# Neighbours on TensorE: linear attention's state products next to its value sums, retention's value sums next to the next pair's scores

## The chip, the cores and the metric

The kernel runs on one core of one Trainium2 chip. A core has a matrix engine (TensorE, PE in the profile), a vector engine (VectorE, DVE), an activation engine (ScalarE, ACT), a general one (GpSimd, POOL) and a queue engine (SyncE, SP), each with its own instruction stream. The metric is the device time of one execution in microseconds (us), the median of the runs.

## The reference

Two layers of a hybrid decoder trunk over 1024 positions of width 1024, all in float32. Each layer makes one projection of the normalised input and cuts it into three head groups: sliding-window attention, retention and gated linear attention. The two that the change touches are recurrences over chunks:

```python
# retention: 4 heads, chunk 128, head width 64
sc = jnp.einsum('bhid,bhjd->bhij', qi, ki) * dmask          # scores
intra = jnp.einsum('bhij,bhjv->bhiv', sc, vi)               # value sums
inter = jnp.einsum('bhid,bhdv->bhiv', qi * q_decay, state)  # inter-chunk product
new_state = chunk_decay * state + jnp.einsum('bhjd,bhjv->bhdv', ki * k_decay, vi)  # state product

# gated linear attention: 4 heads, chunk 64, key width 32, value width 64
sc = jnp.einsum('bhid,bhijd,bhjd->bhij', qi, decay, ki)
intra = jnp.einsum('bhij,bhjv->bhiv', sc, vi)
inter = jnp.einsum('bhid,bhdv->bhiv', qi * jnp.exp(b), state)
new_state = jnp.exp(b_last) * state + jnp.einsum('bhjd,bhjv->bhdv', ki * jnp.exp(b_last - b), vi)
```

Each head's output is RMS-normalised and multiplied by a gate; the three groups are joined, projected by `w_out`, normalised and added to the input.

## The kernel before

The 1024 positions are eight tiles of 128, worked in four pairs (`p` = 0 to 3, tiles 2p and 2p+1). Both recurrences use chunks of 128 positions, one a tile. A projection is a chain of 24 products: the float32 operands are split into two rounded parts and three of their four cross products are summed into one accumulator bank. Most such products have 512 output columns; in the profile they are the groups with output `mm`.

TensorE's order is the program's own. The program is a planner: `mult` issues a product and advances a clock `clk` by its planned cost. The projections are the main line. Everything else is a generator (a "job") that yields a delay, or a delay and the name of a flag; `pump()`, called every few products of a projection, resumes each job whose time has come and whose flag has been set long enough. A job's products so land between the products of a projection. The delays stand in the table `L`, by name and, with `@1`, for layer 1; `lat("rc3", l)` reads one, and `flag(name, lat)` says that something will be ready after `lat`. They order the work and enforce nothing: real waits are semaphores. The other engines' orders come from the framework's scheduler.

Products that don't fill the 128 rows and 128 columns of the array use a part of it: a product over 64 rows (retention's scores, one head each), one with 64 output rows, which uses 64 of the array's columns (`within`, the value sums of retention and of linear attention, and the attention's), one that uses 32 columns (linear attention's state products). The profile shows this as rows*columns: `64*128`, `128*64`, `128*32`.

Accumulators are eight banks: three for projections (`mm()`), five for everything else (`aux()`, 8 - MMB). A bank comes free when its last reader is through. Working tiles in SBUF come from pools too: 14 of width 512 (`t2`) and 7 of width 256 (`t1`).

The functions that the change touches:

- `within(po, i, v, sc)`: four products for one tile, two heads side by side, summed into the output bank `po`. The first starts the bank's accumulation.
- `gla_core` (linear attention, one pair): operands; then the scores of both tiles, masked into `scz`; then the state products `pst`, in 32 columns each; then the delays `gc3` and `gc4`; then the value sums; then for each tile the inter-chunk product (from the state copy `stG`) and VectorE's state update.
- `ret_core` (retention, one pair): waits for the turned operands of both tiles (`rT`), issues the scores of both, VectorE multiplies them with the causal mask into `sc`; after the delay `rc3` come the value sums, and then for each tile the inter-chunk product (from `stR`), the state product and VectorE's update of `stR`; then it starts the output job.
- `ret_out` and `head_norm_gate`: norm and gate of a pair's output from the bank `po`, stored to DRAM for the output projection, which reads it much later.

Lines that the prediction names: L171 every product, L186 every transpose, L147 ScalarE's copies, L967 attention's masked copy out of a score bank, L1253 retention's mask, L1273 and L1275 the update of `stR`, L635 the scaling of the normed input, L1223 the last step of retention's rotation, L1149 to L1166 linear attention's operands.

Of the kernel before, what the change touches and what calls it, by code (L numbers as in the profile page):

```python
# [17 lines left out]
P = 128  # L18
# [4 lines left out]
NP_ = NT // 2  # L23
# [66 lines left out]
def trunk(ctx: ExitStack, tc: tile.TileContext, ins, cst, out):  # L90
# [35 lines left out]
    def aux(dt=F32):  # L126
        return ps.tile([P, 512], dt, tag="aux", name=nm("aux"), bufs=8 - MMB)
# [34 lines left out]
    def h4(ap):  # L162
        return ap.rearrange("p (h q) -> p h q", h=4)
# [640 lines left out]
    stR = cp.tile([P, 2, P], F32, name="stR")  # L804
# [336 lines left out]
    def gla_core(l, p, qk, vs):  # L1141

        yield (lat("gc1", l), ("dec", l, p))
        dA, dB, dC, g = dec[(l, p)]
        flag(("dec0", l, p))
        kxz, kdz, qx, qd, scz = gz["kx"], gz["kd"], gz["qx"], gz["qd"], gz["sc"][p % 2]
        k = qk[:, 256:512]
        a1, ad = t2(), t2()
        V.tensor_tensor(a1, qk, dA, ALU.mult)  # L1149
        V.tensor_tensor(ad, qk, dB, ALU.mult)  # L1150
        q1, k1 = a1[:, 0:256], a1[:, 256:512]
        for s, src in enumerate((dC[:, 0:64], dC[:, 64:192], dC[:, 192:384])):
            n = 8 * s + 8
            eng(f"kd{s}").tensor_tensor(b32(kdz[:, s])[:, :, 0:n], b32(k)[:, :, 0:n],
                                        src.rearrange("p (b i) -> p b i", i=n), ALU.mult)
        kds = [kdz[:, 0], kdz[:, 1], kdz[:, 2], ad[:, 256:512]]
        for s in range(4, 0, -1):
            kv_ = kxz[:, s - 1].rearrange("p c (b i) -> p c b i", i=32)
            eng(f"kx{s}").tensor_tensor(kv_[:, :, 0:s, :], cb32(k1)[:, :, 0:s, :],
                                        g[:, :, 4 * s:5 * s].unsqueeze(3).to_broadcast((P, 2, s, 32)), ALU.mult)  # L1160
        qb = t1()
        eng("qb").tensor_tensor(cb32(qb), cb32(q1), g[:, :, 20:24].unsqueeze(3).to_broadcast((P, 2, 4, 32)), ALU.mult)
        for h in range(4):
            r = slice(32 * h, 32 * h + 32)
# [7 lines left out]
        A.activation(kbn, pt[:, 0:256], AF.Copy)  # L1172
# [12 lines left out]
        pst = aux()  # L1185
        for c in range(2):
            if 2 * p + c < NT - 1:
                for h in range(4):
                    mult(pst[32 * h:32 * h + 32, 64 * c:64 * c + 64], kbn[:, c * P + 32 * h:c * P + 32 * h + 32],
                         vs[c][:, 64 * h:64 * h + 64], True, True, 0.03)  # L1190
        yield lat("gc3", l)
        yield lat("gc4", l)
        po = aux()
        for c in range(2):
            within(po, c, vs[c], scz[c])
        for c in range(2):
            t = 2 * p + c
            if c:
                yield lat("gc6", l)
            if t > 0:  # L1200
                yield (0.0, ("stG", l, t))
            if t > 0:
                for j in range(2):
                    mult(po[:, 256 * j + P * c:256 * j + P * c + P], stG[:, 2 * j:2 * j + 2, :].rearrange("p h d -> p (h d)"),
                         qb[:, c * P:(c + 1) * P], False, c == 1 and j == 1)
            if t < NT - 1:
                V.scalar_tensor_tensor(stC, stC, g[:, c, 24:25], pst[:, 64 * c:64 * c + 64], ALU.mult, ALU.add)
                eng("stx").tensor_tensor(stG, stC.unsqueeze(1).to_broadcast((P, 4, 64)),
                                         hmask.unsqueeze(2).to_broadcast((P, 4, 64)), ALU.mult)
                flag(("stG", l, t + 1), lat("gc5", l))  # L1210
        job(gla_out(l, p, po))
# [26 lines left out]
    def ret_core(l, p, ks, vs):  # L1238
        ts = (2 * p, 2 * p + 1)
        for t in ts:  # L1240
            yield (0.0, ("rT", l, t))
        qT = [turned[(l, t)][:, 0:256] for t in ts]
        kT = [turned[(l, t)][:, 256:512] for t in ts]
        sp = [aux(), aux()]
        for i in range(2):
            for h in range(4):
# [3 lines left out]
        sc = [t2(), t2()]  # L1250
        for i in range(2):
            for c in range(2):
                V.tensor_tensor(h4(sc[i])[:, c:4:2], sp[c][:, 256 * i:256 * i + 256].rearrange("p (h q) -> p h q", h=2),  # L1253
                                causal.unsqueeze(1).to_broadcast((P, 2, P)), ALU.mult)
        yield lat("rc3", l)
        po = aux()
        for i, t in enumerate(ts):
            within(po, i, vs[i], h4(sc[i]))
        for i, t in enumerate(ts):
            if t > 0:  # L1260
                yield (0.0, ("stR", l, t))
            if t > 0:
                for j in range(2):
                    mult(po[:, 256 * j + P * i:256 * j + P * i + P], stR[:, j, :], qT[i][:, j * P:(j + 1) * P], False, i == 1 and j == 1)
            if t < NT - 1:
                pst = aux()
                for j in range(2):
                    mult(pst[:, j * P:(j + 1) * P], ks[i][:, j * P:(j + 1) * P], vs[i][:, j * P:(j + 1) * P],
                         True, True)
                for c in range(2):  # L1270
                    r = slice(64 * c, 64 * c + 64)
                    blk = stR[r, :, 64 * c:64 * c + 64]
                    V.tensor_tensor(blk, blk, pst[r, 0:256].rearrange("p (j n) -> p j n", j=2)[:, :, 64 * c:64 * c + 64],  # L1273
                                    ALU.add)
                V.tensor_tensor(stR, stR, cdt.unsqueeze(2).to_broadcast((P, 2, P)), ALU.mult)  # L1275
                flag(("stR", l, t + 1), lat("rc4", l))
        job(ret_out(l, p, po))

    def ret_out(l, p, po):
# [523 lines left out]
L = {"tt1": 5.86, "tt2": 6.96, "tb1": 28.02, "tb2": 0.05, "pf3": 12.26, "pf1": 6.83, "pf2": 2.88, "mod1": 3.75, "mod2": 2.4, "mod3": 17.58, "mod4": 0.67, "mod5": 0.05, "mod6": 0.05, "pre1": 7.76, "kv1": 15.26, "kv2": 2.17, "aq1": 11.36, "aq7": 4.15, "ag1": 5.72, "aq2": 1.11, "aq6": 7.35, "aq3": 11.35, "aq4": 7.65, "aq5": 2.86, "hn1": 3.34, "hn2": 10.67, "gz1": 9.1, "gz2": 13.49, "gl1": 5.15, "gd3": 17.16, "gc1": 1.82, "gc2": 1.95, "gc3": 0.62, "gc4": 4.49, "gc6": 2.54, "gc5": 4.23, "rc1": 6.33, "rc2": 0.05, "rc3": 1.29, "rc4": 3.27, "fin1": 10.23, "lay1": 0.05, "mod2@1": 2.23, "mod3@1": 15.08, "mod5@1": 2.83, "mod6@1": 3.24, "pre1@1": 10.18, "kv1@1": 4.49, "kv2@1": 0.16, "aq1@1": 6.75, "aq7@1": 7.39, "ag1@1": 10.22, "aq2@1": 2.07, "aq6@1": 9.39, "aq3@1": 11.41, "aq4@1": 6.32, "aq5@1": 1.56, "hn1@1": 4.35, "hn2@1": 9.0, "gz1@1": 5.99, "gz2@1": 8.59, "gl1@1": 20.55, "gd3@1": 15.63, "gc1@1": 2.47, "gc2@1": 4.67, "gc3@1": 0.54, "gc4@1": 0.84, "gc6@1": 1.27, "gc5@1": 0.05, "rc1@1": 5.87, "rc2@1": 2.37, "rc3@1": 2.6, "rc4@1": 5.96, "fin1@1": 6.8, "lay1@1": 0.15, "gc7": 1.43, "gc7@1": 0.05, "tb0": 1.39, "mod7": 1.05, "mod7@1": 1.25}  # L1803
CHUNK = 7
VDB = 8
VDF = 6
# [50 lines left out]
```

## Time and profile before

| | |
|---|---|
| median of 3 runs | 951.92 us (950.53 to 952.58) |
| the profiled execution | 952.01 us |
| its span, first to last instruction | 950.3 us |
| granted TensorE clock, mean | 0.995 |
| TensorE busy | 926.2 us, 97% |
| VectorE, ScalarE, GpSimd busy | 71%, 52%, 24% |

Layer 0's retention stands at about 113 to 205 us of the span, its linear attention at 215 to 300; in layer 1 at 575 to 677 and 677 to 761. In a timeline row a group's length includes the time that its last product takes to pass through the array, so it overlaps the next group; the time from one group's start to the next one's is what the group took of the engine. An idle time in brackets stands with the instruction that ended it.

### The profile page before, as it was taken

The numbers are of one execution on the slowest core, as the hardware profiler recorded it, in microseconds if no ns is written. First come the engines' busy times: TensorE is split into PE (matmuls) and PEld (weight loads), VectorE is DVE, ScalarE is ACT, GpSimd is POOL, SyncE is SP. The second block draws the span as 40 slices with busy tenths as digits, with TensorE's granted clock in tenths as the row PEclk, the third lists the DMA queues.
The fourth block names the chain that finished last, engine by engine and source line by source line (L and its number), as shares of the span: only waits on it lengthen the run. The fifth ranks groups of instructions, "written<-read, shape, count | busy, mean of one in ns | idle before, by whom it ended". The sixth has DMA issues, their size and how long they took to land.

```text
span 950.3 us, 15898 instructions
## 1 busy us (share of the span) xinstructions
PE 926.2 (97%) x5561; PEld 759.8 (80%) x5561; DVE 671.9 (71%) x1426; ACT 496.9 (52%) x1196; POOL 226.7 (24%) x290
## 2 busy tenths in 40 slices
PE   5999999999999999999999999999999999999897
PEld 1699877878898777778889888888889887777685
DVE  6886857848686988655487474784667588678775
ACT  2686333553766766633356441343667577746442
POOL 3222000332240324420123110023233033532000
PEclk8999999999999999999999999999999999999999
DMA  9943623523353245688545251252124133467653
GB/s 329 316 136 104 180 72 124 175 80 112 111 169 112 89 125 178 209 250 280 187 168 184 75 161 60 89 179 88 41 82 124 48 93 99 142 206 224 208 180 111
DMA packets 120206, 140.18 MB, mean 148 GB/s; under 512 B 11727, under 2 KB 86841, under 8 KB 120125
## 3 DMA queue, kind: packets, MB, share of 16 engines
q1 hardware_dynamic: 111964, 129.00, 42.9%
q10 hardware_dynamic: 8160, 10.15, 3.1%
q8 instruction: 44, 0.72, 0.3%
q14 instruction: 38, 0.30, 0.1%
HBM read 105.56 MB, written 33.55 MB: 146 GB/s over the span
## 4 chain that ended last, share of the span: by engine, by line
PE 82%; DMA 6%; DVE 5%; issue 3%; ACT 2%; POOL 1%; SPq 1%; DVEq 0%; POOLq 0%; ACTq 0%
PE mm L171 65%; PE aux L171 13%; PE aux L186 4%; DMA st<-in_w_in_dram 1%; DMA aoS<-t 1%; DMA t<-mixF 1%; DMA xk<-in_x_dram 1%; DMA wm<-in_w_mod_dram 1%; DVE t L339 0%; DMA t<-in_x_dram 0%; DVE arena L1327 0%; POOL arena L509 0%; DMA wide<-in_w_out_dram 0%; ACT smx L972 0%; ACT t L147 0%
## 5 line engine op out<-in xcount | busy, mean ns | idle before, releaser
L171 PE MATMUL mm<-arena,arena 128*128 128x512 f32 (+2 forms) x1392 | 287.5, 359 | 0.0
L171 PE MATMUL mm<-arena 128*128 128x512 f32 (+2 forms) x1392 | 284.6, 358 | 0.3 <-ACT arena L709 0.3
L171 PEld LDWEIGHTS mm<-arena 128*128 128x128 f32 x1392 | 227.4, 189 | 37.7 <-issue 1.2
L171 PEld LDWEIGHTS mm<-arena,arena 128*128 128x128 f32 x1392 | 227.2, 189 | 37.5 <-issue 2.1
L171 PE MATMUL mm<-arena,mx 128*128 128x512 f32 x624 | 146.9, 392 | 2.4 <-ACT wide L1432 2.4
L171 PEld LDWEIGHTS mm<-arena,mx 128*128 128x128 f32 x624 | 115.9, 188 | 27.8 <-ACT wide L1432 2.8
L509 POOL TENSOR_TENSOR arena<-st,arena 128x512 fp32r<-128x512 f32 x53 | 79.9, 1514 | 158.8 <-ACT arena L147 92.2
L147 ACT ACTIVATE t<-aux 128x512 f32<-128x512 f32 x64 | 36.8, 590 | 75.0 <-PE aux L171 36.5
L147 ACT ACTIVATE arena<-st 128x512 fp32r<-128x512 f32 x82 | 48.4, 624 | 31.6 <-PE mm L171 19.8
L972 ACT ACTIVATE smx<-smx,sm 128x129 f32<-128x129 f32 x128 | 50.1, 394 | 21.5 <-DVE sm L969 21.2
L509 DVE TENSOR_TENSOR arena<-st,arena 128x512 fp32r<-128x512 f32 x55 | 54.0, 997 | 7.8 <-ACT arena L147 4.7
L385 DVE SCALAR_TENSOR_TENSOR acc<-st,c_act,acc 128x512 f32<-128x512 f32 x60 | 46.6, 776 | 14.9 <-DMA st<-in_w_mod_dram 13.8
L976 POOL TENSOR_TENSOR smx<-smx,sm 128x512 f32<-128x512 f32 x32 | 35.8, 1118 | 83.2 <-DVE sm L975 79.4
L563 POOL TENSOR_TENSOR sm<-sm,few 128x1 f32<-128x1 f32 x27 | 16.8, 622 | 140.7 <-DVE sm L562 127.6
L186 PE MATMUL aux<-c_ident,t 128*128 128x128 f32 x224 | 34.5, 279 | 4.5 <-DVE t L635 2.7
L967 DVE COPY_PREDICATED smx<-c_curmask,aux 128x256 f32<-128x256 int32 x64 | 25.5, 447 | 14.9 <-ACT smx L147 13.6
L186 PEld LDWEIGHTS aux<-c_ident,t 128*128 128x128 f32 x224 | 27.4, 143 | 10.8 <-DVE t L635 3.2
L371 POOL MEMSET acc<- 128x512 f32 x4 | 2.1, 529 | 133.2 <-PE aux L171 119.1
L1028 DVE TENSOR_TENSOR t<-t,t 128x512 f32<-128x512 f32 x16 | 11.3, 708 | 29.3 <-ACT t L1027 26.2
L852 DVE TENSOR_TENSOR t<-mm,sincos 128x128 f32<-128x128 f32 (+2 forms) x36 | 16.2, 449 | 22.4 <-ACT t L147 12.4
L655 ACT ACTIVATE t<-aux,mod,mod 128x128 f32<-128x128 f32 x56 | 21.2, 455 | 19.5 <-PE aux L186 17.5
L1535 DVE SCALAR_TENSOR_TENSOR t<-t,sm,t 128x512 f32<-128x512 f32 x27 | 20.6, 786 | 13.3 <-DMA t<-in_x_dram 9.5
(278 smaller groups left out, 1479.4 us busy)
## 6 DMA issues: line engine op xcount, KB each, us to landing
st<-in_w_in_dram SPq DMA_DIRECT2D x96, 256.0 KB, 3.2
st<-in_w_mod_dram SPq DMA_DIRECT2D x64, 256.0 KB, 3.6
st<-in_w_out_dram SPq DMA_DIRECT2D x40, 256.0 KB, 3.1
mx<-mixS SPq DMA_DIRECT2D x20, 512.0 KB, 4.9
mixS<-t SPq DMA_DIRECT2D x36, 256.0 KB, 2.2
wm<-in_w_mod_dram SPq DMA_DIRECT2D x12, 512.0 KB, 5.3
t<-in_x_dram SPq DMA_DIRECT2D x24, 256.0 KB, 5.0
t<-tabS SPq DMA_DIRECT2D x16, 256.0 KB, 3.6
```

Source lines behind the costliest of these rows:

```text
L147: A.activation(dst, src, AF.Copy)
L171: T.matmul(dst, lhsT, rhs, start=start, stop=stop, skip_group_check=more)
L186: T.transpose(dst, src, idn)
L385: V.scalar_tensor_tensor(acc, wt, c_act[:, k:k + 1], acc, ALU.mult, ALU.add)
L509: i = (G if first == 0 and kc in LOG else V if first == 0 else eng(f"wlo{kc}")).tensor_tensor(wt[:, 1, 2 * kc:2 * kc + 2, 0:256], st, f(hi ...
L563: after[2] = G.tensor_tensor(r, r, mhalf[:, :w], ALU.pow)
L655: A.activation(hf[:, ks], pt[:, ks], AF.Identity, scale=gain, bias=shift)
L852: V.tensor_tensor(a4, s4, cs.unsqueeze(1).unsqueeze(1).to_broadcast((P, nh, 2, 32)), ALU.mult)
L967: V.copy_predicated(sv, curmask.unsqueeze(1).to_broadcast((P, 2, P)), pv[:, :, n // P - 1, :])
L972: A.activation(sm[:, h, :], sm[:, h, :], AF.Exp, bias=mx[:, h:h + 1], accum_out=sums[:, h:h + 1])
L976: eng("pn").tensor_tensor(sm[:, :, 0:128], sm[:, :, 0:128], rs.unsqueeze(2).to_broadcast((P, 4, P)), ALU.mult)
L1535: V.scalar_tensor_tensor(xt[j], yg[j], r, xt[j], ALU.mult, ALU.add)
```

## The change

In linear attention the state products move from ahead of the delays `gc3` and `gc4` to behind them, directly ahead of the value sums. In retention the value sums of a pair are taken out of its `ret_core`: the output bank is started by the inter-chunk product instead, and the bank, the masked scores and the values are kept in `waiting`. The next pair's `ret_core` issues the kept value sums directly ahead of its own scores; the last pair issues its own after a wait on the flag `rsc`, set `rc3` after the scores. The output job starts after the value sums. No product is added or taken away.

```diff
-    def within(po, i, v, sc):
+    def within(po, i, v, sc, start=True, stop=False):
...
-                     not i and not j, False, 0.108)
+                     start and not i and not j, stop and j == 1, 0.108)
...
@@ gla_core @@
+        yield lat("gc3", l)
+        yield lat("gc4", l)
+        po = aux()
         pst = aux()
         for c in range(2):
             if 2 * p + c < NT - 1:
                 for h in range(4):
                     mult(pst[32 * h:32 * h + 32, 64 * c:64 * c + 64], ...)
-        yield lat("gc3", l)
-        yield lat("gc4", l)
-        po = aux()
         for c in range(2):
             within(po, c, vs[c], scz[c])
...
@@ ret_core @@
         kT = [turned[(l, t)][:, 256:512] for t in ts]
+        if waiting:
+            yield (0.0, ("rsc", l, p - 1))
+            ret_within(l, *waiting.pop())
         sp = [aux(), aux()]
...
-        yield lat("rc3", l)
+        flag(("rsc", l, p), lat("rc3", l))
         po = aux()
-        for i, t in enumerate(ts):
-            within(po, i, vs[i], h4(sc[i]))
+        first = True
         for i, t in enumerate(ts):
             if t > 0:
                 yield (0.0, ("stR", l, t))
             if t > 0:
                 for j in range(2):
-                    mult(po[...], stR[:, j, :], qT[i][...], False, i == 1 and j == 1)
+                    mult(po[...], stR[:, j, :], qT[i][...], first, False)
+                    first = False
...
+        waiting.append((p, po, vs, sc))
+        if p == NP_ - 1:
+            yield (0.0, ("rsc", l, p))
+            ret_within(l, *waiting.pop())
+
+    waiting = []
+
+    def ret_within(l, p, po, vs, sc):
+        for i in range(2):
+            within(po, i, vs[i], h4(sc[i]), False, i == 1)
         job(ret_out(l, p, po))
```

Of the table `L`, these delays change (planner's us). Layer 0, or both layers where there is no entry of its own for layer 1: `tt2` 6.96 to 5.77, `tb1` 28.02 to 32.23, `pf3` 12.26 to 12.47, `pf2` 2.88 to 3.57, `mod3` 17.58 to 14.64, `mod6` 0.05 to 3.45, `kv2` 2.17 to 5.43, `aq1` 11.36 to 11.16, `aq7` 4.15 to 9.71, `ag1` 5.72 to 4.63, `aq3` 11.35 to 10.06, `aq5` 2.86 to 5.44, `gl1` 5.15 to 9.88, `gd3` 17.16 to 18.28, `gc1` 1.82 to 1.11, `gc2` 1.95 to 0.05, `gc4` 4.49 to 4.08, `gc6` 2.54 to 4.36, `gc5` 4.23 to 1.89, `gc7` 1.43 to 5.29, `rc3` 1.29 to 7.11, `rc4` 3.27 to 3.86, `fin1` 10.23 to 10.67. Layer 1: `mod3` 15.08 to 14.9, `aq6` 9.39 to 10.3, `aq4` 6.32 to 5.39, `aq5` 1.56 to 0.88, `hn1` 4.35 to 5.52, `gz2` 8.59 to 8.79, `gc1` 2.47 to 2.11, `rc1` 5.87 to 6.08, `rc2` 2.37 to 0.05, `rc4` 5.96 to 2.92. Unchanged, for reading on: `gc3` 0.62 and, in layer 1, 0.54; `gc4` in layer 1 0.84; `rc3` in layer 1 2.6; `rc2` in layer 0 0.05.

More of the change, by code (lines that the diff above doesn't have):

```diff
@@ L1263, in ret_core @@
                 for j in range(2):
-                    mult(po[:, 256 * j + P * i:256 * j + P * i + P], stR[:, j, :], qT[i][:, j * P:(j + 1) * P], False, i == 1 and j == 1)
+                    mult(po[:, 256 * j + P * i:256 * j + P * i + P], stR[:, j, :], qT[i][:, j * P:(j + 1) * P], first, False)
+                    first = False
             if t < NT - 1:
@@ L1802 @@
 TURN = ("AV", "AV")
-L = {"tt1": 5.86, "tt2": 6.96, "tb1": 28.02, "tb2": 0.05, "pf3": 12.26, "pf1": 6.83, "pf2": 2.88, "mod1": 3.75, "mod2": 2.4, "mod3": 17.58, "mod4": 0.67, "mod5": 0.05, "mod6": 0.05, "pre1": 7.76, "kv1": 15.26, "kv2": 2.17, "aq1": 11.36, "aq7": 4.15, "ag1": 5.72, "aq2": 1.11, "aq6": 7.35, "aq3": 11.35, "aq4": 7.65, "aq5": 2.86, "hn1": 3.34, "hn2": 10.67, "gz1": 9.1, "gz2": 13.49, "gl1": 5.15, "gd3": 17.16, "gc1": 1.82, "gc2": 1.95, "gc3": 0.62, "gc4": 4.49, "gc6": 2.54, "gc5": 4.23, "rc1": 6.33, "rc2": 0.05, "rc3": 1.29, "rc4": 3.27, "fin1": 10.23, "lay1": 0.05, "mod2@1": 2.23, "mod3@1": 15.08, "mod5@1": 2.83, "mod6@1": 3.24, "pre1@1": 10.18, "kv1@1": 4.49, "kv2@1": 0.16, "aq1@1": 6.75, "aq7@1": 7.39, "ag1@1": 10.22, "aq2@1": 2.07, "aq6@1": 9.39, "aq3@1": 11.41, "aq4@1": 6.32, "aq5@1": 1.56, "hn1@1": 4.35, "hn2@1": 9.0, "gz1@1": 5.99, "gz2@1": 8.59, "gl1@1": 20.55, "gd3@1": 15.63, "gc1@1": 2.47, "gc2@1": 4.67, "gc3@1": 0.54, "gc4@1": 0.84, "gc6@1": 1.27, "gc5@1": 0.05, "rc1@1": 5.87, "rc2@1": 2.37, "rc3@1": 2.6, "rc4@1": 5.96, "fin1@1": 6.8, "lay1@1": 0.15, "gc7": 1.43, "gc7@1": 0.05, "tb0": 1.39, "mod7": 1.05, "mod7@1": 1.25}
+L = {"tt1": 5.86, "tt2": 5.77, "tb1": 32.23, "tb2": 0.05, "pf3": 12.47, "pf1": 6.83, "pf2": 3.57, "mod1": 3.75, "mod2": 2.4, "mod3": 14.64, "mod4": 0.67, "mod5": 0.05, "mod6": 3.45, "pre1": 7.76, "kv1": 15.26, "kv2": 5.43, "aq1": 11.16, "aq7": 9.71, "ag1": 4.63, "aq2": 1.11, "aq6": 7.35, "aq3": 10.06, "aq4": 7.65, "aq5": 5.44, "hn1": 3.34, "hn2": 10.67, "gz1": 9.1, "gz2": 13.49, "gl1": 9.88, "gd3": 18.28, "gc1": 1.11, "gc2": 0.05, "gc3": 0.62, "gc4": 4.08, "gc6": 4.36, "gc5": 1.89, "rc1": 6.33, "rc2": 0.05, "rc3": 7.11, "rc4": 3.86, "fin1": 10.67, "lay1": 0.05, "mod2@1": 2.23, "mod3@1": 14.9, "mod5@1": 2.83, "mod6@1": 3.24, "pre1@1": 10.18, "kv1@1": 4.49, "kv2@1": 0.16, "aq1@1": 6.75, "aq7@1": 7.39, "ag1@1": 10.22, "aq2@1": 2.07, "aq6@1": 10.3, "aq3@1": 11.41, "aq4@1": 5.39, "aq5@1": 0.88, "hn1@1": 5.52, "hn2@1": 9.0, "gz1@1": 5.99, "gz2@1": 8.79, "gl1@1": 20.55, "gd3@1": 15.63, "gc1@1": 2.11, "gc2@1": 4.67, "gc3@1": 0.54, "gc4@1": 0.84, "gc6@1": 1.27, "gc5@1": 0.05, "rc1@1": 6.08, "rc2@1": 0.05, "rc3@1": 2.6, "rc4@1": 2.92, "fin1@1": 6.8, "lay1@1": 0.15, "gc7": 5.29, "gc7@1": 0.05, "tb0": 1.39, "mod7": 1.05, "mod7@1": 1.25}
 CHUNK = 7
```

## The prediction

> **What bounds the kernel now.** I read four views: the page's head, TensorE's (PE's) waits away from the two ends, the groups of instructions by shape, and PE's timeline at the places that the change moves.
>
> ```profile
> span 950.3 us, 15898 instructions
> PE 926.2 (97%) x5561; PEld 759.8 (80%) x5561; DVE 671.9 (71%) x1426; ACT 496.9 (52%) x1196; POOL 226.7 (24%) x290
> ```
>
> PE is busy for 97% of the span; the next engine, VectorE (DVE), for 71%. Where does PE wait? From 40 to 880 us:
>
> ```profile
> PE aux L186 <- DVE smx L967: 1.7, 3, 0.9
> PE aux L171 <- ACT t L147: 1.1, 2, 0.6
> PE aux L186 <- DVE t L635: 0.6, 1, 0.6
> PE aux L186 <- DVE t L1223: 0.5, 1, 0.5
> PE aux L171 <- ACT t L1172: 0.2, 1, 0.2
> ```
>
> That is 4.1 us in 840. So no engine feeds PE too slowly; what is left to gain lies inside PE's own stream. The timeline shows it. First retention's last pair in layer 0, then linear attention's first pair in layer 1 (start, length, engine, line, operation, tiles, rows*columns of the array in use, shape, count):
>
> ```profile
> 189.43 0.71 PE L171 MATMUL aux<-t 64*128 64x128 f32 x8
> 190.63 0.71 PE L171 MATMUL aux<-t 64*128 64x128 f32 x8 [0.48 <-ACT t L147]
> 191.28 2.10 PE L171 MATMUL mm<-arena 128*128 128x512 f32 x8
> 193.31 1.09 PE L171 MATMUL aux<-t,t 128*64 128x128 f32 x16
> 194.34 0.71 PE L171 MATMUL aux<-t,stR 128*128 128x128 f32 x4
> 194.88 0.61 PE L171 MATMUL aux<-t,t 128*128 128x128 f32 x4
> 195.25 2.08 PE L171 MATMUL mm<-arena 128*128 128x512 f32 x8
> 197.17 1.98 PE L171 MATMUL mm<-arena,arena 128*128 128x512 f32 x8
> 198.99 0.60 PE L171 MATMUL aux<-t,stR 128*128 128x128 f32 x4
> ...
> 677.86 0.43 PE L171 MATMUL aux<-t,t 128*32 128x64 f32 x16
> 678.22 2.11 PE L171 MATMUL mm<-arena 128*128 128x512 f32 x8
> 680.26 1.10 PE L171 MATMUL aux<-sc,t 128*64 128x128 f32 x16
> ...
> 742.63 0.32 PE L171 MATMUL aux<-t,t 128*32 128x64 f32 x8
> 742.88 2.11 PE L171 MATMUL mm<-arena,arena 128*128 128x512 f32 x8
> ```
>
> I use a group's hold: its start to the next group's start. Eight full-array products with full-array work on both sides hold PE from 197.17 to 198.99, 1.82 us. Eight that stand between a visit to a cut array (64 rows, 64 columns or 32 columns in use) and the next such visit hold it from 191.28 to 193.31 (2.03) and 678.22 to 680.26 (2.04). So leaving one cut and entering another costs a stretch of full-array work 0.22 us, whatever its length. What the change puts side by side no longer pays this.
>
> **How many places.** The groups by shape:
>
> ```profile
> L171 PE MATMUL aux<-t 64*128 64x128 f32 x128 | 9.8, 288 | 1.1 <-ACT t L147 1.1
> L171 PE MATMUL aux<-t,t 128*64 128x128 f32 x128 | 8.8, 279 | 0.0
> L171 PE MATMUL aux<-sc,t 128*64 128x128 f32 x128 | 8.8, 278 | 0.0
> L171 PE MATMUL aux<-t,t 128*32 128x64 f32 x112 | 3.2, 226 | 0.1
> ```
>
> These are retention's scores, its value sums, linear attention's value sums and its state products. At 16 a visit, each of the first three has 8 visits (four pairs in two layers); 112 is six visits of 16 and two of 8, also 8. No matmul is added or removed; only their places change.
>
> **Part 1, retention.** Scores of pair p and value sums of pair p-1 become neighbours for p = 1, 2, 3 in each layer: 6 joins. The scores of pair 0 and the value sums of pair 3 stay alone. A join removes one stretch's 0.22 us; in exchange the value sums are left for the 64-row cut rather than for the full array. The sliding-window attention shows that change already:
>
> ```profile
> 400.54 0.60 PE L171 MATMUL aux<-t,vd 128*64 128x256 f32 x4
> 401.07 1.69 PE L171 MATMUL aux<-kT,mx 64*128 64x256 f32 x24
> 402.69 0.55 PE L186 MATMUL aux<-c_ident,smx 128*128 128x128 f32 x3
> ...
> 315.00 1.69 PE L171 MATMUL aux<-kT,mx 64*128 64x256 f32 x24
> 316.63 0.66 PE L186 MATMUL aux<-c_ident,smx 128*128 128x128 f32 x4
> ...
> 428.08 0.60 PE L171 MATMUL aux<-t,vd 128*64 128x256 f32 x4
> 428.62 1.65 PE L171 MATMUL mm<-arena,mx 128*128 128x512 f32 x6
> ```
>
> Four 64-column products hold PE for 0.53 us before a 64-row group (400.54 to 401.07), and for 0.54 before the full array (428.08 to 428.62). Leaving for rows costs what leaving for the full array costs. The 64-row group then holds 1.62 us, against 1.63 where it comes from the full array (315.00), so nothing is hidden in it. The exchange is even and the gain is 0.22 a join: 6 x 0.22 = 1.3 us (1.2 to 1.5, by the hundredths of the rows).
>
> The join also puts the 1.0 us of value sums (193.31 to 194.34) between retention's turned operands and the scores that read them. Both ScalarE waits on L147 listed above (1.1 us together) are for that copy: one is the 0.48 at 190.63. The longer is 0.6, less than the 1.0 us that now stands ahead of the scores. They go: 1.1 us (0 if another reader takes them over).
>
> **Part 2, linear attention.** The state products move past the two delays to stand directly ahead of the value sums: 8 joins, each without the 0.22 us of the stretch between. What a change from 32 to 64 columns costs, no row shows. Were it free, the state products would also lose their exit: 16 hold 0.36 and 8 hold 0.25 (742.63 to 742.88), so 8 more cost 0.11, and the fixed part is 0.14; the gain would be 0.22 + 0.14 = 0.36. Were it to cost that 0.14 a second time on top of an exit, the gain would be 0.08. The nearest row, columns to rows, costs what an exit costs (0.53 against 0.54); I take that, 0.22: 8 x 0.22 = 1.8 us, ends 0.6 and 2.9. The Trainium skill, "TensorEngine Tiling (Array Packing)", Tiling Modes, says that a change of mode drains the array while a change of tile within a mode does not, and lists 32 and 64 columns as two configurations: by it the free end is out. By it this term stays at 1.8 and cannot be 2.9.
>
> VectorE's state update reads the moved products, but it rewrites the tile that the next inter-chunk product reads and so already waits for that product, which comes after the value sums (about 1.0 us); it is not made late.
>
> **Part 3, what moves later.** Retention's output work for a pair (a gate load on ScalarE's queue, five ScalarE and four VectorE operations, one sum product pair on PE, two stores to `mixS` on SP's queue) starts one pair later, 18 to 29 us; for pair 3 it starts after the delay `rc3`, 7.11 instead of 1.29 in layer 0. Its reader is the output projection, whose first product starts at 403.5 in layer 0:
>
> ```profile
> L171 PE MATMUL mm<-arena,mx x624: 387/389/499, 403.5 to 940.7; 128*128 128x512 f32 x156
> ```
>
> Retention's last product of layer 0 starts at 198.99 (above), 200 us ahead of it: hidden, cost 0. Layer 1 has the same order and is taken alike.
>
> The retention state stage now follows the scores at once. Its update on VectorE queues behind the four masks:
>
> ```profile
> 191.38 1.42 DVE L1253 TENSOR_TENSOR t<-aux,c_causal 128x256 f32<-128x256 f32 x4 [1.07 <-PE aux L171]
> 195.53 0.59 DVE L1273 TENSOR_TENSOR stR<-stR,aux 64x128 f32<-64x128 f32 x2 [2.74 <-PE aux L171]
> 196.15 0.42 DVE L1275 TENSOR_TENSOR stR<-stR,c_cdt 128x256 f32<-128x256 f32 x1
> ```
>
> The masks end 1.5 us after the scores' hold ends; the state products end 0.9 to 1.2 us after it. The update then takes 1.0 us, so it starts only some 0.3 to 0.6 us later after its products than now. Its reader, the pair's second inter-chunk product, has 198.99 - 196.57 = 2.4 us in hand, and `rc4` grows in layer 0. In layer 1 `rc4` falls by 3.04. A delay counts in planner's time, in which a 512-column product is 0.213 us against 0.2275 here, so the product comes up to 3.2 us earlier; a place with no more than 2.4 us in hand would wait 0.8. Three of the four such products in layer 1 may have more in hand; I take one wait of 0.5, between 0 and 0.8.
>
> **Part 4, the other delays.** They move small groups among the projections; a group costs the same wherever it stands alone, so they cost only waits. `aq3` in layer 0 falls by 1.29, `gc1` plus `gc2` by 2.61, `rc2` in layer 1 by 2.32 (covered by the value sums now ahead of the scores, except at pair 0). What covers them is the projections, of which PE always has some at hand: it waited 4.1 us in all. Taken as 0, ends +1.5 and -2.8 (the waits on L967, L635 and L1223 gone).
>
> **Sum.** 1.3 + 1.1 + 1.8 - 0.5 = 3.7 us. The profiled execution took 952.0 us (span 950.3 and 1.7 around it), which is within 0.1 of the median of the three runs, 951.92. 952.0 - 3.7 = 948.3 us.
>
> **Rivals.** *Slower: the accumulator banks run out.* The pool `aux` has 5 banks. Retention's output bank is now opened at the state products and kept until the next pair's value sums and their norm are through. At the state products of pairs 1 to 3 five are alive: the kept one, two of scores, the new output and the state product's. Any sixth (a turn, a modulation sum) makes PE wait until the masks free the scores: 1.5 us after the scores, when PE wants the bank 0.54 us after them (194.34 to 194.88), so 1.0 us, with all projections queued behind. Six times is 6.0 us: 948.3 + 6.0 = 954.3. It decides above 3.7 / 6 = 0.6 us a pair. For it: the wait on L967 is PE waiting for VectorE to leave a score bank, up to 0.9 us, where attention holds four. Against it: all other users are read by one ScalarE or VectorE operation within about a microsecond. The Trainium skill, "PSUM — Partial Sum Buffer", Summary: rules for kernel authors, says to evacuate promptly because the memory is tight; by that rule this case would be the likeliest. The trace agrees only at L967.
>
> *No change that can be measured.* The 32-to-64 change is at its dear end (0.6 us), the new wait at 0.8, and the ScalarE waits only move to another reader: 1.3 + 0.6 - 0.8 = 1.1, 950.9 us. For it: nothing shows the 32-to-64 change. Against it: the change between two other cuts is no dearer than an exit.
>
> *More than forecast.* The 32-to-64 change is free (2.9), no new wait, and the new delays also clear the 2.8 us on L967, L635 and L1223: 1.3 + 1.1 + 2.9 + 2.8 = 8.1, 943.9 us.
>
> **How the numbers follow.** A measurement of this kernel tells about 0.2%, 1.9 us, from no change: faster means below 950.0, slower above 953.8. Forecast 0.52, with its own range from 1.3 + 1.1 + 0.6 - 0.8 = 2.2 to 1.5 + 1.1 + 2.9 = 5.5, 946.5 to 949.8; more than that 0.13; no change 0.22; banks 0.13. Faster 0.65, same 0.22, slower 0.13. The range 945.3 to 953.0 leaves out the banks and the far half of the gain.
>
> **What the next profile would show.** Right: `aux<-t,t` 128*64 followed at once by `aux<-t` 64*128 six times, and 128*32 by 128*64 eight times; no wait on L147 before scores; the state products' 0.36 hold unchanged. Wrong: a PE wait on L1253 at the state products (banks), on L1275 at the second inter-chunk product (delay), or on L1149 to L1166 at linear attention's scores (`gc1`, `gc2`); or a hold of the joined groups 0.2 us longer than the sum of the two.

## The result and the profile after

The changed kernel takes 944.5 us (median of four runs, 942.9 to 946.6) against 952.1 for the kernel before on the same chip: a ratio of 0.9926, interval 0.9911 to 0.9941. Two later comparisons on other chips gave 0.9925 (0.9901 to 0.9948) and 0.9926 (0.9904 to 0.9947). The forecast was 948.3 with a range of 945.3 to 953.0; the gain is 7.6 us, twice the 3.7 forecast. The profiled execution took 945.7 us with a span of 944.0.

The head of the page of the changed kernel, the counterpart of the first lines shown of before:

```profile
span 944.0 us, 15922 instructions
PE 922.4 (98%) x5561; PEld 760.4 (81%) x5561; DVE 675.9 (72%) x1426; ACT 499.1 (53%) x1198; POOL 228.6 (24%) x290
```

PE's busy time falls by 3.8 us, the span by 6.3: some 2.5 us came out of waiting. PE's waits of the changed kernel from 40 to 880 us (in all, times, longest):

```profile
PE aux L171 <- DVE t L1021: 2.3, 1, 2.3
PE aux L186 <- DVE t L635: 0.6, 1, 0.6
PE mm L171 <- ACT arena L661: 0.2, 1, 0.2
```

L967, L147, L1223 and L1172 are gone, and one new wait of 2.3 us stands on L1021, retention's head norm. The same view for the tail, 880 to 960 us, first the kernel before (two lines), then the changed one:

```profile
PE mm L171 <- ACT wide L1432: 2.4, 1, 2.4
PE mm L171 <- DVE t L1413: 0.8, 1, 0.8
```

```profile
PE mm L171 <- ACT wide L1445: 0.7, 1, 0.7
```

The forecast stopped reading at 880 us and so left out these 3.2 us, of which 2.5 went. (Behind the moved code the lines of the changed kernel have other numbers: L1253 became L1256, L1275 became L1278, L1413 and L1432 became L1426 and L1445.)

The new neighbours are in PE's timeline of the changed kernel as foreseen, value sums with scores six times and state products with value sums eight times:

```profile
134.30 1.09 PE L171 MATMUL aux<-t,t 128*64 128x128 f32 x16
135.32 1.16 PE L171 MATMUL aux<-t 64*128 64x128 f32 x16
136.41 0.38 PE L171 MATMUL aux<-t,stR 128*128 128x128 f32 x1
...
678.24 0.43 PE L171 MATMUL aux<-t,t 128*32 128x64 f32 x16
678.60 1.10 PE L171 MATMUL aux<-sc,t 128*64 128x128 f32 x16
679.63 2.13 PE L171 MATMUL mm<-arena 128*128 128x512 f32 x8
```

The value sums hold PE for 1.02 us ahead of the scores (134.30 to 135.32), as they did ahead of the full array. The state products hold 0.36 ahead of the value sums (678.24 to 678.60), exactly what they held ahead of the full array, and the value sums 1.03. So the change from 32 to 64 columns, which no row of before showed, costs what an exit costs, the middle that the forecast took. The Trainium skill, "TensorEngine Tiling (Array Packing)", Tiling Modes, treats these as two configurations with a drain between them; the trace agrees (0.36 in both places).

Counted over PE's whole timeline after the first 34 us, the changes between array cuts fall from 155 to 141, by just the 14 joins. Two of the 155 stand at a wait and are counted with the stalls; the other 153 cost 18.5 us, the 141 cost 16.1. All PE stalls together, the small ones that the waits do not list too, fall from 9.6 to 4.8 us. Against that, one stretch of products at half clock (a granted clock of 0.51) adds 1.4 us. That is 2.4 + 4.8 - 1.4 = 5.8 of the 6.3 us.

### The profile page after: what moved, and what is told of

It is laid out like the page before. It is cut to its first block, busy times and chain, and to the rows that moved or that the text cites. A ratio compares the mean times of both kernels' runs of the same rounds, so it can differ in the third digit from the quotient of the medians.

```text
span 944.0 us, 15922 instructions
## 1 busy us (share of the span) xinstructions
PE 922.4 (98%) x5561; PEld 760.4 (81%) x5561; DVE 675.9 (72%) x1426; ACT 499.1 (53%) x1198; POOL 228.6 (24%) x290
## 5 line engine op out<-in xcount | busy, mean ns | idle before, releaser
L509 POOL TENSOR_TENSOR arena<-st,arena 128x512 fp32r<-128x512 f32 x53 | 79.0, 1499 | 149.3 <-ACT arena L147 93.0
L147 ACT ACTIVATE t<-aux 128x512 f32<-128x512 f32 x64 | 36.9, 589 | 62.7 <-PE aux L186 37.7
L147 ACT ACTIVATE arena<-st 128x512 fp32r<-128x512 f32 x82 | 47.9, 626 | 36.4 <-PE mm L171 19.2
L509 DVE TENSOR_TENSOR arena<-st,arena 128x512 fp32r<-128x512 f32 x55 | 57.5, 1066 | 6.1 <-PE mm L171 3.2
L385 DVE SCALAR_TENSOR_TENSOR acc<-st,c_act,acc 128x512 f32<-128x512 f32 x60 | 48.2, 803 | 17.1 <-DMA st<-in_w_mod_dram 15.9
L967 DVE COPY_PREDICATED smx<-c_curmask,aux 128x256 f32<-128x256 int32 x64 | 25.5, 446 | 12.0 <-ACT smx L147 9.7
L655 ACT ACTIVATE t<-aux,mod,mod 128x128 f32<-128x128 f32 x56 | 21.2, 456 | 22.3 <-PE aux L186 16.2
L987 POOL TENSOR_SCALAR_AFFINE_SELECT t<-t 128x512 f32<-128x512 f32 x28 | 22.3, 806 | 41.7 <-ACT t L147 38.2
L1548 DVE SCALAR_TENSOR_TENSOR t<-t,sm,t 128x512 f32<-128x512 f32 x27 | 20.8, 785 | 16.2 <-DMA t<-in_x_dram 10.4
```

The costliest lines, as they stand in the source:

```text
L147: A.activation(dst, src, AF.Copy)
L385: V.scalar_tensor_tensor(acc, wt, c_act[:, k:k + 1], acc, ALU.mult, ALU.add)
L509: i = (G if first == 0 and kc in LOG else V if first == 0 else eng(f"wlo{kc}")).tensor_tensor(wt[:, 1, 2 * kc:2 * kc + 2, 0:256], st, f(hi ...
L655: A.activation(hf[:, ks], pt[:, ks], AF.Identity, scale=gain, bias=shift)
L967: V.copy_predicated(sv, curmask.unsqueeze(1).to_broadcast((P, 2, P)), pv[:, :, n // P - 1, :])
L987: G.affine_select(h4(pr), h4(pf), [[0, 4], [1, P]], ALU.is_ge, 0.0, base=0, channel_multiplier=-1)
```

## The experiments

The theory before them: the new neighbours give some 3 us, the vanished ScalarE waits 1.1, and the rest comes from waits that the new delays cleared. The rival: the two moves themselves clear the waits, and the delays are worth nothing, as the forecast had it.

### The new order with the old delays (e1_struct)

```
 after.py, with
-L = { ... the new table ... }
+L = { ... the table of before ... }
```

> The changed kernel with the whole delay table of before. Theory (neighbours 4 us, delays the rest): 14 joins at 0.22 us and the ScalarE waits of 1.1 before retention's scores give 3 to 4.5 us under the kernel before, about 948 us, and the waits at attention (L967) and in the last output stage stay. Rival (the moved products do it all, the delays nothing): as the changed kernel, 943 to 945 us. Rival (delays do it all): within 1 us of before.

Measured: 965.8 us, ratio 1.0149 (1.0127 to 1.0171): 14 us **slower** than before. The order alone is a loss: the rival falls, and so does the theory, which had it at 948. The cut changes are as cheap as in the changed kernel (142 of them, 16.2 us), but stalls are 19.1 us against 4.8, and stretches at half clock add 8.4. Its longest waits from 40 to 960 us:

```profile
PE aux L186 <- DVE smx L967: 6.1, 2, 4.2
PE aux L186 <- DVE mx L1159: 2.9, 1, 2.9
PE mm L171 <- ACT wide L1445: 1.9, 1, 1.9
PE aux L186 <- DVE t L1223: 1.5, 1, 1.5
PE aux L171 <- ACT mx L1165: 1.1, 1, 1.1
```

VectorE's timeline of this kernel shows where the 2.9 us on L1159 come from:

```profile
225.48 0.75 DVE L385 SCALAR_TENSOR_TENSOR acc<-st,c_act,acc 128x512 f32<-128x512 f32 x1 [2.91 <-DMA st<-in_w_mod_dram]
...
232.48 0.75 DVE L385 SCALAR_TENSOR_TENSOR acc<-st,c_act,acc 128x512 f32<-128x512 f32 x1 [2.76 <-DMA st<-in_w_mod_dram]
...
235.16 0.94 DVE L1149 TENSOR_TENSOR t<-t,t 128x512 f32<-128x512 f32 x1
236.03 0.94 DVE L1150 TENSOR_TENSOR t<-t,t 128x512 f32<-128x512 f32 x1
236.89 1.15 DVE L1159 TENSOR_TENSOR mx<-t,gs 128x256 f32<-128x256 f32 x2
```

The operands of linear attention's second pair (L1149 to L1159) stand in VectorE's queue behind the modulation's sums (L385), which wait for their weights, up to 2.9 us each. PE's timeline has the other side:

```profile
231.63 3.13 PE L171 MATMUL mm<-arena,arena 128*128 128x512 f32 x13
237.62 0.44 PE L186 MATMUL aux<-c_ident,mx 128*128 128x128 f32 x2 [2.86 <-DVE mx L1159]
239.14 2.90 PE L171 MATMUL aux<-mx,mx 128*128 128x128 f32 x12 [1.09 <-ACT mx L1165]
```

PE asks for them at 234.8, before VectorE has begun them. In the changed kernel the same operand stands behind shorter waits for weights (1.3 and 0.9 us) and ahead of the last sum:

```profile
224.52 0.68 DVE L1149 TENSOR_TENSOR t<-t,t 128x512 f32<-128x512 f32 x1
...
227.62 0.75 DVE L385 SCALAR_TENSOR_TENSOR acc<-st,c_act,acc 128x512 f32<-128x512 f32 x1
```

It is made from 224.5 on, and PE takes it without a wait at 236.4.

The longest wait of the order with the old delays, 4.2 us on L967, comes about in the same way. VectorE, then PE:

```profile
388.51 0.75 DVE L385 SCALAR_TENSOR_TENSOR acc<-st,c_act,acc 128x512 f32<-128x512 f32 x1 [3.68 <-DMA st<-in_w_mod_dram]
389.18 0.77 DVE L967 COPY_PREDICATED smx<-c_curmask,aux 128x256 f32<-128x256 int32 x2
...
389.67 0.69 PE L186 MATMUL aux<-c_ident,smx 128*128 128x128 f32 x2 [4.19 <-DVE smx L967]
```

Attention's copy out of the score bank stands right behind a sum that waits 3.68 us for its weight. In the changed kernel no wait of L385 from 340 to 430 us is longer than 0.4 us. The two kernels below that repeat these waits have the late weight too (3.7 us in e4 and 4.0 in e9, with waits on L967 of 2.5 and 4.3 behind it). The other wait of e1 on L967 (1.9 us, at 323.2) has no wait for a weight ahead of it.

### The old order with the new delays (e2_delays)

```
 before.py, with the new value of every key of L but gc* and rc*
```

> The kernel before with the new delays, except those of the two recurrences (gc and rc), which keep their old values. Theory: the joins are missing, but the attention waits on L967, the one on L1223 and most of the last output stage's 3.2 us go: 3 to 5 us under before, about 948 us. Rival (the moved products do it all): within 1 us of before.

Measured: 954.1 us, 1.0034 (1.0019 to 1.0049), 3 us slower, where 948 was expected. Its waits on L147 rise to 2.5 us in four. Neither part gains by itself: +14 and +3, and the whole change -7.6. (The two parts are not quite the whole: the old order with the new `gc` and `rc` too was not run.)

### Linear attention's move alone (e3_gla)

```
+        yield lat("gc3", l)
+        yield lat("gc4", l)
+        po = aux()
         pst = aux()
         ...  (the state products)
-        yield lat("gc3", l)
-        yield lat("gc4", l)
-        po = aux()
```

In before.py, with its delays.

> The kernel before with the linear attention part alone (state products behind the two delays), old delays. Theory: 8 joins at 0.22 us, 1.8 us under before (0.19%). Were the change from 32 to 64 columns free: 2.9. If only waits counted and not the neighbours: 0.

Measured: 951.6 us, 1.0008 (0.9995 to 1.0021): no change. What the changes between cuts cost falls by 1.3 us, of the 1.8 expected; a new wait on L1021 of 1.9 us at 240 takes them back.

### Retention's move alone (e4_ret)

```
+        if waiting:
+            yield (0.0, ("rsc", l, p - 1))
+            ret_within(l, *waiting.pop())
         sp = [aux(), aux()]
 ...  (the rest of the diff in retention; linear attention as before, delays of before)
```

> The kernel before with the retention part alone, old delays. Theory: 6 joins at 0.22 us and two ScalarE waits of 1.1 us: 2.4 us under before. Rival (accumulator banks run out at the state products): 3 to 4 us over before, with PE waits on the mask line.

Measured: 961.7 us, 1.0116 (1.0096 to 1.0137), 10 us slower. It has the waits of e1 (L967 5.6 us in two, L1159 1.8), so it is this move that upsets the order. PE waits neither on the masks (L1256 here) nor on the state (L1278), so there is no sign of the banks running out.

### Which delays repair it (e5_newgr, e6_newrest, e9_rc3, e10_gc, e11_mod, e13_gc7, e14_gcrest, e15_old7)

All have the new order. A value in brackets is the one that was replaced.

```
e5_newgr    old table, but new gc* and rc*
e6_newrest  new table, but old gc* and rc*
e9_rc3      old table, but rc3 = 7.11 (1.29)
e10_gc      old table, but new gc*
e11_mod     old table, but new mod3, mod6
e13_gc7     old table, but gc7 = 5.29 (1.43)
e14_gcrest  old table, but new gc* without gc7
e15_old7    new table, but gc7 = 1.43 (5.29)
```

> The changed kernel's order with the new delays of the two recurrences alone (gc and rc), the others as before. The order with all old delays was 14.6 us slower than before. Theory (the recurrences' own delays repair what the moved products push late): the waits at linear attention's operands (L1159, L1165), L858 and L1223 go, those on L967 stay; 948 to 956 us. Rival (the delays of the rest repair it): 960 us or more.

> The complement: the changed kernel's order with all new delays except gc and rc, which are the old ones. Theory: the waits at linear attention's operands stay (5 to 8 us with the lower clock after them), those on L967 go; 950 to 960 us. Rival (the rest repairs it): 943 to 946 us.

> The changed order with all old delays, but for rc3 of layer 0 (7.11 for 1.29). All old delays gave 965.8, all new 944.5. Theory A (with the short rc3, retention's last value sums and their norm come onto VectorE's and ScalarE's queues just ahead of linear attention's first two pairs, whose operands then queue behind modulation's weight loads): this one delay gives back most of it, about 953 (950 to 957), linear attention's second operand (L1149) starts near 220 to 225 again instead of 235.7, and the waits on L1159 and L1165 go. Theory B (it is linear attention's own delays): stays at 963 to 966. Theory C (no single delay does it; each place in the order counts): between, 957 to 963.

> The changed order with all old delays, but for those of linear attention (gc1, gc2, gc4 to gc7, both layers). Theory A (rc3 is what repairs): stays near 962 (959 to 966), the operand L1149 still near 235. Theory B (linear attention's own delays repair, gc1 plus gc2 falling by 2.61 above all): about 950 to 954, no waits on L1159 and L1165. Theory C: between.

> The changed order with all old delays, but for those of the modulation (mod3 and mod6 of layer 0, mod3 of layer 1 by 0.18). In the two kernels with retention moved and old delays, VectorE stood 6.5 to 6.8 us between 224 and 234 us in L385 for weight loads, with linear attention's operands queued behind. Theory D (those loads, put into VectorE's queue too early, are what costs): 952 to 957, and the stand in L385 falls under 3 us. Theories A and B: 962 to 967, since mod3 and mod6 come after those products. In the kernel with only retention's and linear attention's delays new the same stand is 5.1 us and it takes 949.2, which speaks against D.

> The changed order with all old delays, but for gc7 of layer 0 (5.29 for 1.43). Theory G (one delay: gc7 stands between the scores of a pair's two tiles and so puts off all later work of linear attention in layer 0 by up to 3.9 us a pair; with the old value PE comes to the second pair's operands 2.9 us before VectorE has made them, at 234.8 against 237.6): close to what the whole set gave, 950 to 953, no wait on L1159. Theory H (gc1 and gc2 falling, or all together): 958 to 966, the wait on L1159 stays.

> The changed order with all old delays, but for linear attention's delays other than gc7. Theory G: 962 to 968 (gc1 plus gc2 falls by 2.6, so PE comes to the operands earlier still, and the wait on L1159 stays or grows). Theory H: 950 to 956.

> The changed kernel with gc7 of layer 0 at its old 1.43. Theory G: clearly slower than 944.5, 950 to 956, with a wait of 2 us or more at linear attention's operands (L1159, L1172 or L1165) in layer 0. Theory H: 944 to 947.

Measured:

| kernel | us | ratio to before | interval |
|---|---|---|---|
| e5_newgr | 949.2 | 0.9990 | 0.9978 to 1.0001 |
| e6_newrest | 954.2 | 1.0034 | 1.0020 to 1.0048 |
| e9_rc3 | 964.7 | 1.0138 | 1.0120 to 1.0156 |
| e10_gc | 950.4 | 0.9993 | 0.9982 to 1.0005 |
| e11_mod | 956.9 | 1.0058 | 1.0039 to 1.0077 |
| e13_gc7 | 966.1 | 1.0168 | 1.0142 to 1.0195 |
| e14_gcrest | 957.8 | 1.0080 | 1.0059 to 1.0101 |
| e15_old7 | 963.7 | 1.0148 | 1.0125 to 1.0171 |

Against e1's 965.8: linear attention's delays give back 15 us, the modulation's 9, retention's rc3 about 1, which is within the intervals. So theory A of these texts (rc3 repairs) fell. B (linear attention's own delays) and D (the modulation's) each hold in part. e10 makes the second pair's operand at 217.6, ahead of the weights that come late (2.1, 1.0 and 1.9 us from 226 on). In e11 only one weight comes late there, by 1.7 us, and the operand follows it at 224.8. In neither does PE wait on L1159 any more; the wait of 4.2 us on L967 has gone in both too, and with it the wait for a weight ahead of it. That two unrelated sets of delays both take these waits away is what ties them to the order in VectorE's queue; what the waits are worth within the 15 and the 9 us was not measured apart. e6, with the new delays but the recurrences' old ones, stays 3 us above before; its longest wait is one of 2.7 us on L1172.

The single-delay theory G fell too. gc7 alone gives nothing (966.1), although its wait on L1159 is gone; the others without it give 8, all together 15; and the old gc7 in the otherwise new table costs 19 us. The stall does not go, it changes its place and its operand. The longest waits of PE between 230 and 250 us, from the timelines of e13, e14 and e15 in this order:

```profile
244.49 1.52 PE L171 MATMUL aux<-t,bones 128*128 128x512 f32 x2 [5.63 <-ACT t L147]
```

```profile
238.40 1.65 PE L171 MATMUL aux<-mx,mx 128*128 128x128 f32 x6 [4.15 <-ACT mx L1166]
```

```profile
241.42 0.98 PE L171 MATMUL aux<-mx,mx 128*128 128x128 f32 x6 [4.15 <-ACT mx L1166]
```

All three lie where e1 waits for linear attention's second pair, but it is head norm's input that is late in the first and ScalarE's copies of the pair's operands (L1166) in the others. e15 has a further wait of 4.2 us on L1159, at 291.8. The delays act as a set. The rest of the new table, on top of gc and rc, is worth 949.2 - 944.5 = 4.7 us by the medians: e5 still has 1.5 us of waits on L967, 0.9 on L147 and 2.2 in the tail, with a stretch at half clock behind the last.

### The neighbours separated again (e8_split)

```
             (the state products)
+        yield 0.05
         for c in range(2):
             within(po, c, vs[c], scz[c])
 ...
             ret_within(l, *waiting.pop())
+            yield 0.05
         sp = [aux(), aux()]
```

In after.py: some work from another job comes between the neighbours, nothing else is asked for.

> The changed kernel with the neighbours parted again: one delay of 0.05 between the state products and the value sums in linear attention, and between the value sums and the next scores in retention, so a few projection products stand between them; all else as in the changed kernel. Theory (being neighbours is worth 0.2 us a join): 14 joins, 2.4 to 3.1 us over the changed kernel, about 947 us. Rival (only the time at which they are issued counts): as the changed kernel, 943 to 946.

Measured: 952.0 us, 1.0014 (1.0002 to 1.0025), 7.5 us slower than the changed kernel, where 2.4 to 3.1 were expected. Its timeline at one place:

```profile
683.66 0.43 PE L171 MATMUL aux<-t,t 128*32 128x64 f32 x16
684.02 1.21 PE L171 MATMUL mm<-arena 128*128 128x512 f32 x4
685.17 1.10 PE L171 MATMUL aux<-sc,t 128*64 128x128 f32 x16
```

Four full-array products hold PE for 1.15 us between the two cuts (684.02 to 685.17), where at 0.2275 each they are 0.91: 0.24 more. Over the whole timeline the changes rise from 141 to 157 and cost 3.2 us more, 0.20 each against the 0.22 of the forecast. The price of a neighbour is right. The other 4.3 us are in part stalls: they are 8.1 for 4.8 us, while the 1.4 us at half clock are gone, and some 2 us of the difference are not placed. 14 delays of 0.05 were enough to bring back waits on L147 (1.7 us in three).

### The wait that is left (e7_hn, e12_after, e16_wlo, e17_wlo, e18_after)

The changed kernel's runs fall into two groups, so one place may go either way. These five ask whether it is the wait on L1021.

```
e7_hn       after.py, hn1 = 5.0 (3.34)
e12, e18    after.py as it is
e16, e17    after.py, EN["wlo3"] = "V" ("G"): half of L509 from GpSimd to VectorE
```

> The changed kernel with layer 0's delay hn1 at 5.0 instead of 3.34, so that the head norm's sum product comes two pump steps later. In its profile PE waited 2.3 us on L1021 there, and ran five products at half clock behind it. Theory (that wait is what separates the changed kernel's runs at 943 from those at 946): 941.5 to 943.5 us, no wait on L1021. Rival (the spread has another source): 943 to 946.

> The changed kernel again, beside the three others. If its gain is no matter of the chip: ratio 0.991 to 0.995, 943 to 947. Its runs spread over 3.7 us so far; theory: one place, the update behind L1021 at 168 us, costs 2.3 us and 1.4 us of half clock in some executions and not in others. Then a profile in a run near 943 shows no L1021 wait of over 1 us, one near 946 shows it.

> The changed kernel with half of L509 (the low halves of the weights with kc 3) taken from GpSimd to VectorE, where one takes 1.07 us in the mean against 1.50 on GpSimd. If VectorE's two slow steps ahead of the wait at 168 us (L1278 1.51 and L1021 1.74) come from running beside GpSimd, these go back to 0.42 and 0.69, and the wait of 2.3 us with its 1.4 us of half clock goes: 941 to 943. But VectorE gets about 26 x 1.07 = 28 us of new work in its queue, and waits have moved elsewhere in each try so far: 946 to 950 if it does here too.

> The changed kernel with half of L509 on VectorE, again, now on one chip with the changed kernel. Theory (it takes away the half-clock stretch behind the L1021 wait, which the changed kernel has in about half of its executions): all runs 942 to 944.5, median 1.5 to 3 us under the changed kernel's, its low group being no lower than these. Rival (the chip of the last call was the faster one): the same median within 1 us.

> The changed kernel, beside it. Theory: two groups again, near 942.5 and 946.3, median between 943 and 946.5. Rival: one group at 942 to 944.

Measured: e7 947.4 us (0.9963, 0.9948 to 0.9978), not the 941.5 to 943.5 expected: the wait on L1021 goes, one of 2.2 us on L1030 comes at 315.6. e12 945.7, e18 944.3. Fifteen runs of the changed kernel give 941.4 to 943.3 (seven) and 945.7 to 946.7 (eight). The profiles of 945.7 and 946.7 have the wait at 2.3 and 2.5 us; e18's profile fell at 942.1. The two timelines, PE and then VectorE and GpSimd; first the run of 945.7:

```profile
168.38 0.77 PE L171 MATMUL aux<-t,bones 128*128 128x512 f32 x1 [2.33 <-DVE t L1021]
168.94 1.91 PE L171 MATMUL mm<-arena 128*128 128x512 f32 x4
...
164.47 0.75 DVE L385 SCALAR_TENSOR_TENSOR acc<-st,c_act,acc 128x512 f32<-128x512 f32 x1 [1.41 <-DMA st<-in_w_mod_dram]
165.14 1.51 DVE L1278 TENSOR_TENSOR stR<-stR,c_cdt 128x256 f32<-128x256 f32 x1
166.58 1.74 DVE L1021 TENSOR_TENSOR t<-t,t 128x512 fp32r<-128x512 f32 x1
...
164.75 3.03 POOL L509 TENSOR_TENSOR arena<-st,arena 128x512 fp32r<-128x512 f32 x2 [15.65 <-ACT arena L147]
```

and e18, the run of 942.1:

```profile
166.25 0.50 PE L171 MATMUL aux<-t,bones 128*128 128x512 f32 x1 [0.79 <-DVE t L1021]
166.59 1.09 PE L171 MATMUL mm<-arena 128*128 128x512 f32 x4
...
163.42 0.75 DVE L385 SCALAR_TENSOR_TENSOR acc<-st,c_act,acc 128x512 f32<-128x512 f32 x1 [0.97 <-DMA st<-in_w_mod_dram]
164.09 0.42 DVE L1278 TENSOR_TENSOR stR<-stR,c_cdt 128x256 f32<-128x256 f32 x1
164.42 1.78 DVE L1021 TENSOR_TENSOR t<-t,t 128x512 fp32r<-128x512 f32 x1
...
164.17 3.18 POOL L509 TENSOR_TENSOR arena<-st,arena 128x512 fp32r<-128x512 f32 x2 [15.65 <-ACT arena L147]
```

If the modulation's weight comes half a microsecond late, VectorE starts L1278 after GpSimd has begun L509 and takes 1.51 us instead of 0.42, and then L1021 takes 1.74 as well. If it comes in time, only L1021 is caught before PE needs it. PE waits 2.33 us in the one and 0.79 in the other, and in the first the clock falls. Two windows, the changed kernel's and then e18's (stretch, length, busy time and count of PE, PEld, DVE, ACT and POOL, granted clock, DMA share, GB/s):

```profile
168.40:171.80 3.40, 3.40 (x11) 2.94 (x12) 1.80 (x4) 2.03 (x3) 0.00 (x0) 0.51 0.42 122
```

```profile
166.50:169.90 3.40, 3.40 (x20) 2.92 (x20) 3.32 (x7) 3.08 (x4) 0.85 (x1) 1.00 0.35 85
```

Eleven products fall into the one, 20 into the other. The wait and its clock together cost 1.5 + 1.4 = 2.9 of the 3.6 us between the two runs.

With one of the two L509 there moved to VectorE, e16 shows L1021 back at 0.68 and no half clock; PE still waits 1.25 us on it (0.94 in e17):

```profile
164.38 1.51 DVE L1278 TENSOR_TENSOR stR<-stR,c_cdt 128x256 f32<-128x256 f32 x1
165.81 0.68 DVE L1021 TENSOR_TENSOR t<-t,t 128x512 fp32r<-128x512 f32 x1
...
163.99 1.62 POOL L509 TENSOR_TENSOR arena<-st,arena 128x512 fp32r<-128x512 f32 x1 [15.65 <-ACT arena L147]
```

Measured: e16 942.6 us (0.9921, 0.9901 to 0.9942), and in a second comparison, e17, 942.5 (0.9915, 0.9897 to 0.9933) beside e18's 944.3 on the same chip. Its eleven runs lie between 941.9 and 944.1, none in the upper group. The median is 1.7 us under the changed kernel's, as expected, but the intervals of the two ratios overlap. So it takes the upper group away, and does not lower the fastest runs; it is at least as fast as the changed kernel.

## Why the prediction was wrong

**Part 4, the other delays, is the step that failed.** It said that a group costs the same wherever it stands, that PE always has projections at hand, and so "Taken as 0, ends +1.5 and -2.8"; its end of +1.5 had no row behind it. The runs show 21 us between the old and the new delays in the new order (965.8 against 944.5). The argument was read from the waits of before, an order in which operands happened to be early. It held for PE's work and not for VectorE's queue: in e1 the operands behind a sum that waits for a weight came late by 2.9 and 4.2 us, and no stock of projections helps once PE's own order has come to them. The part also named the wrong delays: `gc1`, `gc2` and `aq3` as they bring work forward, and not `gc7` in layer 0, which grows by 3.86 us and whose old value costs 19 us. That the zero was not further off is luck: in the profiled execution the waits on L967, L1223 and L1172 that went (2.4 us) stand against the new one on L1021 and its half clock (3.7).

**The waits were cut off at 880 us.** The tail's 3.2 us were neither in the sum nor in any range; 2.5 of them went.

**A wait was priced at its own length.** The one of 2.3 us cost another 1.4 in clock, and in e1 the stretches at half clock cost 8.4.

What held: the price of a neighbour (0.20 a change against 0.22), the 32-to-64 change at the cost of an exit, and the two ScalarE waits on L147, which went. All 14 joins came; at 0.20 they are some 2.8 us, against 1.3 + 1.8 = 3.1. The wait on the retention state (Part 3, 0.5 us) did not come in the changed kernel; e6 has one of 0.8 us on L1278.

The rivals: the banks did not run out, in the changed kernel or in e4, where no other delay helps. "No change" did not come. "More than forecast" (943.9) is nearest in time and right that the waits on L967 and L1223 would be cleared; it put the rest on a free change of columns, which is not free, and the wait on L635 (0.6) stayed.

What stays open: e13 to e15 were read at one wait each and not followed back through all queues, so that a wait for a weight lies behind their stalls is not shown; how the 21 us divide among the waits is not either; and 0.5 of the 6.3 us of span are not placed.

## What to carry to other kernels

Where work is ordered by a table of delays, a move and the table are one change: neither can be costed without the other, and a forecast for a move with newly set delays needs a range that allows for all waits to go and for new ones as large as the old. For each operand that moves, look in the queue of the engine that makes it for what stands ahead and can wait for a load. Read PE's waits to the very end of the span.

## What was not expected of the hardware

**A wait costs more than itself.** In all traces together (from 40 us to 12 us before the end), no PE wait under 1.6 us brought half clock by itself. Of those between 1.8 and 3.2 us 16 of 27 did, mostly for 3.4 us, as in the window above (0.51); the wait of 2.4 us in the tail of before did not. Those over 4 us always did, for 6.8 us in all but one. In e1 behind the wait on L1159:

```profile
238.00:244.80 6.80, 5.71 (x21) 5.14 (x21) 6.70 (x19) 4.83 (x12) 2.19 (x3) 0.50 0.08 19
```

Which waits do it can be read from the traces too. In each trace every change of the granted clock lies on a grid of 3.413 us. Over the same stretches, PE's idle time was summed in each cell of this grid that ran at full clock. The clock fell behind 22 cells, with 1.80 to 2.91 us idle; it fell behind none with less, and of those with more only two, with 1.89 and 1.92, did not bring it down. So a wait counts by what of it falls into one cell: the 2.33 us of the changed kernel lie in one, the 2.39 us in the tail of before in two, 1.39 in the first.

The Trainium skill, "TensorE: Matmul & The Clock Gate", What's actually happening, describes a free-running window of about 3.4 us. The 3.4 and 6.8 us agree, and so does it that the same wait may or may not be hit. It gives an idle window of 3.4 us as the condition; here 1.8 to 2.9 us idle within a window were enough, and the measurement decides.

**VectorE stands still beside GpSimd.** L1278 takes 0.42 us where it begins ahead of L509 and 1.51 where it begins behind, L1021 0.68 alone and 1.74 behind (lines above), so about 1.1 us more, while GpSimd's two take 3.03 us. The Trainium skill, "SBUF — State Buffer", Who interferes with whom, says that a VectorE instruction with two inputs there and a GpSimd instruction that reads it exclude each other, and the later one waits. The trace agrees: in the run of 945.7 the first L509 ends at 166.37 and L1278 at 166.66, the second at 167.78 and L1021 at 168.32. Each ends after the one it met, though by less than it takes alone (0.28 for 0.42 us, 0.55 for 0.68).
